# Order of the plain loads in the dense stage of an encoder block: raw second weights first, raw first weights one iteration behind the split, gate blocks by halves

## The chip, the cores and the metric

The kernel runs on one core of a Trainium2 chip. The metric is the device time of one execution in microseconds (us). PE is TensorE, DVE VectorE, ACT ScalarE, POOL GpSimd and SP SyncE; SP computes nothing here, it issues plain loads and stores as DMAs, one after the other in program order.

## What is computed

The reference is one encoder block over 1024 tokens of width 1024: a norm, a projection, attention beside a depthwise convolution, an output projection, and then an expert layer that the change is about. Its core is this:

```python
q = (xc @ peer_wq).reshape(TOKEN_CHUNK, PEER_HEADS, PEER_DQ)
...
v1, i1 = lax.top_k(s1, PEER_TOPK)
v2, i2 = lax.top_k(s2, PEER_TOPK)
...
g = jax.nn.softmax(top_s, axis=-1).astype(xc.dtype)
u = peer_u[e]
h = jax.nn.gelu(jnp.einsum('cd,chkd->chk', xc, u))
return jnp.einsum('chk,chkd->cd', g * h, peer_v[e])
```

Every token picks 128 of 16384 experts. An expert has a row of `peer_u` (the first weights), whose product with the token goes through a gelu and is scaled by a gate, and a row of `peer_v` (the second weights) that is added with this factor. All is float32; products on PE are made of three matmuls each on a rounded high part and a low rest of both operands.

## The kernel before

Of the eight tiles of 128 tokens, three are done by gathering: POOL fetches for each of the 128 choices of a tile the rows of `peer_u`, later of `peer_v`, by an indirect DMA (L1162, 512 KB each) into one of seven slots, and DVE works a slot off with one instruction (L1195 for the dot products, L1207 for the sums). A slot is fetched anew when DVE is done with it. The other five tiles (640 tokens) are done densely, over all 128 chunks of 128 experts. For chunk i:

- first product: PE multiplies the chunk of first weights with the normed tokens (`uhalf`, L1504) into the bank `hps`, ACT makes the gelu (L1514) into a buffer `ho`. The raw weights `ur` are loaded by `uload` (L1226) into one of two buffers and split by `usplit` (L1236): ACT makes the high part `uh` (L116), POOL the rest `ul` (L119). For 33 of the chunks this product was made earlier; their `ho` is loaded by `hload` (L1481).
- gate: DVE multiplies `ho` with the gate block `gl`, in two halves of the tokens (`amake1`, L1487); ACT rounds it to `ah` (L1489), DVE makes the rest `al` (L1495). A gate block holds four chunks and comes in two halves of 640 KB (`gload`, L1461), which share three buffers.
- second product: `vload` (L1465) loads the raw second weights `vr` into one of two buffers, `vsplit` has ACT make `vh` (L116) and POOL `vl` (L119); PE multiplies `ah`, `al` with them (L122 to L124). Four of the ten output blocks stay in PSUM banks (`acc`), the other six go in turns of two chunks through one bank `prot`, from which DVE adds to `X` (L1569).

The dense stage is the loop `for i in range(NK - 1)` at L1608, 127 iterations. The order within an engine is that of the program's text; each engine waits on semaphores for what an instruction needs. So SP issues the loads strictly in order, and a load whose buffer is not free yet holds up those behind it. Iteration i emits the loads for chunk i + 2, splits the second weights of chunk i + 1, and splits first weights in three of four iterations. The calls stand like this, with the gate block inside `loads` ahead of `vload` every fourth time, and the next `uload` inside `uahead`, behind the split that frees its buffer:

```python
            loads(i + 2)
            vsplit(nx)
            uahead()
```

Of the kernel before, what the change touches and what calls it, by code (L numbers as in the profile page):

```python
# [31 lines left out]
NK = 128  # L32
# [8 lines left out]
GCH = 4  # L41
# [30 lines left out]
def peer_block(tc, I, out):  # L72
# [1151 lines left out]
    def uload(i):  # L1224
        raw = uu.tile([P, DC, P], F32, name="ur", tag="raw", bufs=2)
        SY.dma_start(raw[:], I["peer_uT"][i])  # L1226
        RAW["u", i] = raw
# [4 lines left out]
    def usplit(i):  # L1232
        raw = RAW.pop(("u", i))
        uh = uu.tile([P, DC, P], F32R, name="uh", tag="uh", bufs=2)
        ul = uu.tile([P, DC, P], F32R, name="ul", tag="ul", bufs=2)
        split(uh[:], ul[:], raw[:], hi_eng=HE(i), lo_eng=V if i in UI and UI[i] > KM else G)  # L1236
        UW[i] = (uh, ul)
# [189 lines left out]
    with ExitStack() as vs:  # L1427
# [27 lines left out]
        AL = {}  # L1455
        HO = {}

        def gload(i):
            for hf in range(2):
                gl[i, hf] = vp.tile([P, NB2, GCH, TB], F32, name="gl", tag="gl", bufs=3)  # L1460
                SY.dma_start(gl[i, hf][:], GD[hf * NB2:(hf + 1) * NB2, :, i:i + GCH, :].rearrange("b p i t -> p b i t"))  # L1461

        def vload(i):
            raw = vp.tile([P, D], F32, name="vr", tag="vr", bufs=RB)
            SY.dma_start(raw[:], I["peer_v"][i * P:(i + 1) * P, :])  # L1465
            RAW["v", i] = raw

        def vsplit(i):
            raw = RAW.pop(("v", i))
            vh = vp.tile([P, D], F32R, name="vh", tag="vh", bufs=WIN + 1)  # L1470
            vl = vp.tile([P, D], F32R, name="vl", tag="vl", bufs=WIN + 1)
            split(vh[:], vl[:], raw[:], lo_eng=G)
            CH[i] = (vh, vl)
# [4 lines left out]
        def hload(i):  # L1478
            if i in UI and i not in HO and i < NK:
                HO[i] = hfree.pop(0)  # L1480
                SY.dma_start(HO[i], HDm[UI[i]])  # L1481

        def amake1(i):
            ho = HO[i]
            for hf in range(2):
                o = ho[:, hf * HT_:(hf + 1) * HT_].rearrange("p (b t) -> p b t", t=TB)
                V.tensor_tensor(o, o, gl[i - i % GCH, hf][:, :, i % GCH, :], op=ALU.mult)  # L1487
            ah = vp.tile([P, TD], F32R, name="ah", tag="ah", bufs=WIN + 1)
            A.copy(ah[:], ho)  # L1489
            AL[i] = ah  # L1490

        def amake2(i):
            ho = HO.pop(i)
            al = vp.tile([P, TD], F32R, name="al", tag="al", bufs=WIN + 1)
            V.tensor_tensor(al[:], ho, f(AL[i][:]), op=ALU.subtract)  # L1495
            AL[i] = (AL[i], al)
            hfree.append(ho)

        def uhalf(i, hf, ps, d0=0, d1=DC):
            a, b = segs[hf]  # L1500
            uh, ul = UW[i]
            for dc in range(d0, d1):
                for st3 in range(3):
                    PE.matmul(ps[:, :b - a], (uh, uh, ul)[st3][:, dc, :], HN[(0, 1, 0)[st3]][:, dc, a:b],  # L1504
                              start=dc == 0 and st3 == 0, stop=dc == DC - 1 and st3 == 2)
            if hf and d1 == DC:
                UW.pop(i)

        def ubank():
            return psv.tile([P, 512], F32, name="hps", tag="h", bufs=1)  # L1510

        def ugelu(ho, hf, ps):
            a, b = segs[hf]
            A.activation(ho[:, a:b], ps[:, :b - a], AF.Gelu_apprx_tanh)  # L1514

        def loads(i):
            if 0 <= i < NK:
                if i % GCH == 0:
                    gload(i)
                vload(i)  # L1520


        ulist = [i for i in range(NK) if i not in UI]
        ug = dict(g=0, split=0, load=0, ps=None)

        def uahead():
            m = ug["g"] // 4
            if ug["split"] < min(m + 2, len(ulist)):
                usplit(ulist[ug["split"]])
                ug["split"] += 1  # L1530
                if ug["load"] < len(ulist):
                    uload(ulist[ug["load"]])
                    ug["load"] += 1

        def ugroup():
            m, q = divmod(ug["g"], 4)
            if m >= len(ulist):
                return
            i, (hf, d) = ulist[m], divmod(q, 2)
            if ug["split"] <= m:  # L1540
                uahead()
            if d == 0:
                ug["ps"] = ubank()
            uhalf(i, hf, ug["ps"], d * DC // 2, (d + 1) * DC // 2)
            if d == 1:
                if hf == 0:
                    HO[i] = hfree.pop(0)
                ugelu(HO[i], hf, ug["ps"])
            ug["g"] += 1

        def uready(i):
            while i not in UI and ulist.index(i) >= ug["g"] // 4:
                ugroup()
# [4 lines left out]
        def rotate(w, i, wide):  # L1558
            t, n = rot[w]
            todo = list(range(last[w] + 1, i + 1))  # L1560
            last[w] = i
            if not todo:
                return
            pr = (ubank() if wide else psv.tile([P, 512], F32, name="prot", tag="r", bufs=1))[:]
            for c in todo:
                ah, al, vh, vl = *AL[c], *CH[c]
                mm3(pr, ah[:, t * P:(t + 1) * P], al[:, t * P:(t + 1) * P], vh[:, n:n + 512],
                    vl[:, n:n + 512], c == todo[0], c == i)
            V.tensor_tensor(X[:, NG + t, n:n + 512], X[:, NG + t, n:n + 512], pr, op=ALU.add)  # L1569
# [8 lines left out]
        ug["load"] = 2  # L1578
        hload(0)
        loads(0)  # L1580
        loads(1)
        for i in range(KM, K0):
            if i + 1 < K0:
                usplit(US[i + 1])
            else:
                amake1(0)
                amake2(0)
                vsplit(0)
                uahead()
            ho = vp.tile([P, TD], F32, name="hm", tag="al", bufs=WIN + 1)[:]  # L1590
            for hf in range(2):
                hps = ubank() if hf == 0 else psv.tile([P, 512], F32, name="prot", tag="r", bufs=1)
                uhalf(US[i], hf, hps)
                ugelu(ho, hf, hps)
            SY.dma_start(HDm[i], ho)

        def accum(i, js):
            ah, al, vh, vl = *AL[i], *CH[i]
            for j in js:
                t, n = pers[j]  # L1600
                mm3(acc[j][:], ah[:, t * P:(t + 1) * P], al[:, t * P:(t + 1) * P], vh[:, n:n + 512],
                    vl[:, n:n + 512], i == 0, i == NK - 1)
# [5 lines left out]
        for i in range(NK - 1):  # L1608
            nx = i + 1
            ng = gat0 + -(-(ngat - gat0) * min(nx, nb) // nb) - gat.nc  # L1610
            gs = [0] * 3
            for j in range(ng):
                gs[SPOTS[j % len(SPOTS)]] += 1
            hload(nx)
            if len(hfree) > 1:
                hload(i + 2)
            loads(i + 2)
            vsplit(nx)
            uahead()
            rs_ = [w for w in range(len(rot)) if i % WIN == w % WIN]  # L1620
            rotate(rs_[0], i, False)
            accum(i, (0,))
            ugroup()
            gat.adv(gs[0])
            rotate(rs_[1], i, False)
            accum(i, (1,))
            ugroup()
            uready(nx)
            amake1(nx)
            gat.adv(gs[1])  # L1630
            amake2(nx)
            rotate(rs_[2], i, False)
            accum(i, (2, 3))
            ugroup()
            gat.adv(gs[2])
            CH.pop(i - WIN, None)
# [72 lines left out]
```

## Time and profile before

| what | value |
|---|---|
| median of three runs | 2976.93 us (2971.88 to 2979.38) |
| the profiled execution's own time | 2979.52 us |
| span of its trace | 2977.7 us |
| busy: PE, DVE, POOL, ACT | 94%, 81%, 64%, 39% |
| moved by DMA | 710.33 MB, mean 239 GB/s |
| the dense stage in the trace | from about 1360 to 2950 us |

The shares are over the whole span, in which stages with different limits follow each other; for the dense stage the rows below are taken from its own stretch. "Busy" of PE counts matmuls whose ends are modelled, so its pace is read better from the starts of its rows.

### The profile page before, as it was taken

The numbers are of one execution on the slowest core, as the hardware profiler recorded it, in microseconds if no ns is written. First come the engines' busy times: TensorE is split into PE (matmuls) and PEld (weight loads), VectorE is DVE, ScalarE is ACT, GpSimd is POOL, SyncE is SP. The second block draws the span as 40 slices with busy tenths as digits, with TensorE's granted clock in tenths as the row PEclk, the third lists the DMA queues.
The fourth block names the chain that finished last, engine by engine and source line by source line (L and its number), as shares of the span: only waits on it lengthen the run. The fifth ranks groups of instructions, "written<-read, shape, count | busy, mean of one in ns | idle before, by whom it ended". The sixth has DMA issues, their size and how long they took to land.

```text
span 2977.7 us, 44502 instructions
## 1 busy us (share of the span) xinstructions
PE 2799.5 (94%) x16042; PEld 2477.2 (83%) x16048; DVE 2424.8 (81%) x4465; ACT 1166.3 (39%) x2408; POOL 1916.8 (64%) x1526
## 2 busy tenths in 40 slices
PE   7988899999999899978999999999999999999997
PEld 6867787798988788857888888888888888888886
DVE  4889877458666977766899988999889989898998
ACT  3237666243577577672222222222222222222222
POOL 2667741104446666765777777878777878787775
PEclk9999999899999999999999999999999999999999
DMA  3121000154345667668989898999989998999896
GB/s 124 53 76 36 1 15 1 53 161 122 96 149 181 224 219 251 235 238 299 342 331 350 328 348 331 345 342 352 337 319 337 344 343 336 347 336 339 332 342 227
DMA packets 296719, 710.33 MB, mean 239 GB/s; under 512 B 25264, under 2 KB 135216, under 8 KB 296368
## 3 DMA queue, kind: packets, MB, share of 16 engines
q0 software_dynamic: 110592, 402.70, 35.3%
q1 hardware_dynamic: 156800, 252.85, 25.2%
q10 hardware_dynamic: 29104, 51.91, 4.7%
q8 instruction: 126, 2.06, 0.3%
q14 instruction: 97, 0.79, 0.1%
HBM read 640.46 MB, written 66.91 MB: 238 GB/s over the span
## 4 chain that ended last, share of the span: by engine, by line
PE 53%; DVE 20%; DMA 11%; issue 7%; ACT 4%; POOL 4%; ACTq 1%; SPq 0%; POOLq 0%; DVEq 0%
PE hps L1504 13%; PE hps L1244 5%; PE prot L122 4%; PE prot L123 4%; PE prot L124 4%; DMA rows<-peer_u,ei 4%; PE pg L1108 3%; DMA rows<-peer_v,ei 2%; PE acc L124 2%; PE acc L122 2%; PE acc L123 2%; DMA vr<-peer_v 2%; DVE ga L1207 2%; DVE ho L1487 2%; DMA GD<-gblk 2%
## 5 line engine op out<-in xcount | busy, mean ns | idle before, releaser
L1504 PE MATMUL hps<-HN,uh 128*128 128x320 f32 x3072 | 682.8, 309 | 9.3 <-ACT ho L1251 5.3
L1504 PEld LDWEIGHTS hps<-HN,uh 128*128 128x128 f32 x3072 | 530.3, 188 | 42.7 <-issue 5.5
L1504 PE MATMUL hps<-HN,ul 128*128 128x320 f32 x1536 | 475.4, 309 | 0.6 <-POOL ul L119 0.6
L1207 DVE SCALAR_TENSOR_TENSOR ga<-rows,aa,ga 128x1024 f32<-128x1024 f32 x330 | 423.8, 1284 | 30.1 <-DMA rows<-peer_v,ei 23.6
L1162 POOL DMA_INDIRECT rows<-peer_u,ei x339 | 362.4, 1069 | 108.0 <-issue 56.3
L119 POOL TENSOR_TENSOR vl<-vr,vh 128x1024 fp32r<-128x1024 f32 x128 | 308.9, 2413 | 153.3 <-ACT vh L116 110.7
L1162 POOL DMA_INDIRECT rows<-peer_v,ei x330 | 325.2, 985 | 112.9 <-issue 64.5
L1195 DVE SCALAR_TENSOR_TENSOR QB<-rows,ga 128x1024 bf16<-128x1024 f32 x271 | 329.4, 1216 | 29.8 <-DMA rows<-peer_u,ei 25.5
L122 PE MATMUL prot<-vh,ah 128*128 128x512 f32 x762 | 308.8, 405 | 30.4 <-DVE X L1569 27.9
L119 POOL TENSOR_TENSOR ul<-ur,uh 128x1024 fp32r<-128x1024 f32 x127 | 323.0, 2543 | 2.6
L1569 DVE TENSOR_TENSOR X<-X,prot 128x512 f32<-128x512 f32 x384 | 261.9, 682 | 68.6 <-PE prot L124 66.4
L123 PE MATMUL prot<-vl,ah 128*128 128x512 f32 x762 | 301.0, 395 | 0.4 <-POOL vl L119 0.4
L124 PE MATMUL prot<-vh,al 128*128 128x512 f32 x762 | 297.4, 390 | 0.0
L1504 PEld LDWEIGHTS hps<-HN,ul 128*128 128x128 f32 x1536 | 289.1, 188 | 0.9 <-POOL ul L119 0.9
L1514 ACT ACTIVATE ho<-hps 128x320 f32<-128x320 f32 x128 | 55.9, 437 | 487.2 <-PE hps L1504 487.2
L1118 ACT COPY gblk<-pg 128x128 f32<-128x128 f32 x640 | 176.0, 441 | 100.6 <-PE pg L1108 71.4
L116 ACT CAST vh<-vr 128x1024 fp32r<-128x1024 f32 x128 | 133.7, 1045 | 201.7 <-DMA vr<-peer_v 201.7
L1244 PE MATMUL hps<-HN,uh 128*128 128x320 f32 x992 | 210.8, 335 | 0.0
L124 PE MATMUL acc<-vh,al 128*128 128x512 f32 x512 | 199.8, 390 | 0.0
L122 PE MATMUL acc<-vh,ah 128*128 128x512 f32 x512 | 199.8, 390 | 0.0
L123 PE MATMUL acc<-vl,ah 128*128 128x512 f32 x512 | 199.7, 390 | 0.0
L122 PEld LDWEIGHTS prot<-vh,ah 128*128 128x128 f32 x762 | 143.0, 188 | 67.9 <-DVE X L1569 47.6
(276 smaller groups left out, 6502.9 us busy)
## 6 DMA issues: line engine op xcount, KB each, us to landing
ur<-peer_uT SPq DMA_DIRECT2D x128, 512.0 KB, 4.4
vr<-peer_v SPq DMA_DIRECT2D x128, 512.0 KB, 7.8
GD<-gblk ACTq DMA_DIRECT2D x80, 512.0 KB, 5.1
gl<-GD SPq DMA_DIRECT2D x64, 640.0 KB, 7.7
wqr<-peer_wq SPq DMA_DIRECT2D x32, 512.0 KB, 3.9
HDm<-ho SPq DMA_DIRECT2D x31, 320.0 KB, 2.9
s<-SD SPq DMA_DIRECT2D x64, 128.0 KB, 3.0
ho<-HDm SPq DMA_DIRECT2D x22, 320.0 KB, 5.0
```

What stands on the lines that cost most here:

```text
L116: A.copy(hi, src)
L119: lo_eng.tensor_tensor(lo, src, f(hi), op=ALU.subtract)
L122: PE.matmul(ps, ah, bh, start=start, stop=False)
L123: PE.matmul(ps, ah, bl, start=False, stop=False)
L124: PE.matmul(ps, al, bh, start=False, stop=stop)
L1118: A.copy(gblk[b][k][:, :, q * 4:q * 4 + 4].rearrange("p i t -> p t i"), pg[:, :, k * w:k * w + w])
L1162: G.indirect_dma_start(out=r, out_offset=None, in_=I["peer_v" if ph else "peer_u"], in_offset=bass.IndirectOffsetOnAxis(ap=ge[t][:, k:k + ...
L1195: V.scalar_tensor_tensor(jk, r, 1.0, h, op0=ALU.mult, op1=ALU.mult, accum_out=self.hh[t][:, k:k + 1])
L1207: V.scalar_tensor_tensor(to, r, self.aa[t][:, k:k + 1], to, op0=ALU.mult, op1=ALU.add)
L1244: PE.matmul(hps[:, j, :b - a], (uh, uh, ul)[st3][:, dc, :], HN[(0, 1, 0)[st3]][:, dc, a:b], start=dc == 0 and st3 == 0, stop=dc == DC - 1 ...
L1504: PE.matmul(ps[:, :b - a], (uh, uh, ul)[st3][:, dc, :], HN[(0, 1, 0)[st3]][:, dc, a:b], start=dc == 0 and st3 == 0, stop=dc == DC - 1 and ...
L1569: V.tensor_tensor(X[:, NG + t, n:n + 512], X[:, NG + t, n:n + 512], pr, op=ALU.add)
```

## The change

The instructions are the same, and so is their order on PE, DVE, ACT and POOL (rows differ only in line numbers and in the numbers of buffers). Only the order of SP's loads differs. The second weights now come ahead of the `hload` for chunk i + 2. The first weights have a call of their own, `uloads()`, ahead of the iteration's splits, where the buffer it needs was freed by a split of an earlier iteration. The gate block is loaded by halves, called behind the `amake1` of the last chunk of a block: then come the second half of the next block and the first half of the one after it. Two more calls, each one half, go ahead of the loop.

```diff
-        def gload(i):
-            for hf in range(2):
+        def gload(i, hf):
+            if i < NK:
                 gl[i, hf] = vp.tile([P, NB2, GCH, TB], F32, name="gl", tag="gl", bufs=3)
                 SY.dma_start(gl[i, hf][:], GD[hf * NB2:(hf + 1) * NB2, :, i:i + GCH, :].rearrange("b p i t -> p b i t"))
...
         def loads(i):
             if 0 <= i < NK:
-                if i % GCH == 0:
-                    gload(i)
                 vload(i)
...
             if ug["split"] < min(m + 2, len(ulist)):
                 usplit(ulist[ug["split"]])
                 ug["split"] += 1
-                if ug["load"] < len(ulist):
-                    uload(ulist[ug["load"]])
-                    ug["load"] += 1
+
+        def uloads():
+            if ug["load"] < min(ug["split"] + 2, len(ulist)):
+                uload(ulist[ug["load"]])
+                ug["load"] += 1
...
         hload(0)
         loads(0)
+        gload(0, 0)
+        gload(0, 1)
         loads(1)
+        gload(GCH, 0)
...
             hload(nx)
+            loads(i + 2)
             if len(hfree) > 1:
                 hload(i + 2)
-            loads(i + 2)
+            uloads()
             vsplit(nx)
             uahead()
...
             amake1(nx)
+            if nx % GCH == GCH - 1:
+                gload(nx + 1, 1)
+                gload(nx + 1 + GCH, 0)
             gat.adv(gs[1])
```

Within the loop, SP's order repeats every four iterations. `vr` are raw second weights, `ur` raw first weights, `gl` halves of gate blocks, `ho` or `QB` a first product made earlier. Before, one such period late in the stage stands like this:

```order
L1226 DMA ur<-peer_uT 128x1024
L1481 DMA ho_14274<-HDm 128x640
L1465 DMA vr<-peer_v 128x1024
L1461 DMA gl<-GD 128x10x128 x2
L1465 DMA vr<-peer_v 128x1024
L1226 DMA ur<-peer_uT 128x1024
L1465 DMA vr<-peer_v 128x1024
L1226 DMA ur<-peer_uT 128x1024
L1465 DMA vr<-peer_v 128x1024
```

And now, in the same place:

```order
L1465 DMA vr<-peer_v 128x1024
L1481 DMA ho_14274<-HDm 128x640
L1226 DMA ur<-peer_uT 128x1024
L1465 DMA vr<-peer_v 128x1024
L1461 DMA gl<-GD 128x10x128 x2
L1465 DMA vr<-peer_v 128x1024
L1226 DMA ur<-peer_uT 128x1024
L1465 DMA vr<-peer_v 128x1024
L1226 DMA ur<-peer_uT 128x1024
```

The `vr` directly behind the two `gl` used to be that of the chunk that opens the new gate block; it now stands ahead of them, and the one behind them is that of the next chunk. The two `gl` were the halves of one block and are now the second half of it and the first half of the block after it.

Ahead of the loop, SP's order before was this (`HDm<-hm` are stores of first products that are made there):

```order
L1226 DMA ur<-peer_uT 128x1024
L1481 DMA ho_14273<-HDm 128x640
L1461 DMA gl<-GD 128x10x128 x2
L1465 DMA vr<-peer_v 128x1024 x2
L1595 DMA HDm<-hm 128x640
L1226 DMA ur<-peer_uT 128x1024
L1595 DMA HDm<-hm 128x640
L1481 DMA ho_14274<-HDm 128x640
```

It is now:

```order
L1226 DMA ur<-peer_uT 128x1024
L1481 DMA ho_14273<-HDm 128x640
L1465 DMA vr<-peer_v 128x1024
L1461 DMA gl<-GD 128x10x128 x2
L1465 DMA vr<-peer_v 128x1024
L1461 DMA gl<-GD 128x10x128
L1598 DMA HDm<-hm 128x640 x2
L1481 DMA ho_14274<-HDm 128x640
```

One `vr` moved ahead of the first gate block, half a gate block was added ahead of the stores, and the `ur` between the stores left this place for one inside the loop.

## Rows read from the trace of the kernel before

**Rows 1.** Windows: length, busy time by engine, clock, DMA share, GB/s; one stretch.

```profile
1900.00:2000.00 100.00, 99.97 (x539) 88.72 (x538) 91.59 (x139) 24.29 (x35) 79.93 (x60) 1.00 0.93 343
```

**Rows 2.** Windows of iterations 106 to 109 and 111, from first acc matmul to the next.

```profile
2690.64:2702.78 12.14, 12.14 (x68) 10.90 (x67) 10.27 (x12) 2.19 (x4) 10.15 (x8) 1.00 0.77 277
2702.78:2715.03 12.25, 12.25 (x68) 10.90 (x66) 11.38 (x11) 4.37 (x7) 8.42 (x6) 1.00 0.89 343
2715.03:2728.03 13.00, 12.62 (x67) 10.90 (x66) 12.07 (x13) 3.14 (x5) 11.00 (x10) 1.00 0.93 346
2728.03:2740.18 12.15, 12.15 (x68) 10.90 (x67) 11.15 (x13) 2.36 (x4) 9.14 (x8) 1.00 1.02 380
...
2752.32:2766.06 13.74, 12.65 (x67) 10.82 (x66) 12.87 (x11) 4.71 (x7) 8.40 (x6) 1.00 0.81 308
```

**Rows 3.** Timeline of PE in iteration 106: start, us, tile.

```profile
2691.32 0.45 PE L1504 MATMUL hps<-HN,uh 128*128 128x320 f32 x2
...
2693.07 0.39 PE L122 MATMUL prot<-vh,ah 128*128 128x512 f32 x1
...
2695.14 0.45 PE L1504 MATMUL hps<-HN,uh 128*128 128x320 f32 x2
```

**Rows 4.** Timeline of SP: start, us including the wait; first, typical and last gate blocks.

```profile
1370.27 25.23 SPq L1461 DMA_DIRECT2D gl<-GD  x2
...
2674.33 22.11 SPq L1461 DMA_DIRECT2D gl<-GD  x2
2696.53 0.60 SPq L1465 DMA_DIRECT2D vr<-peer_v  x1
2697.24 0.38 SPq L1226 DMA_DIRECT2D ur<-peer_uT  x1
2697.66 0.67 SPq L1465 DMA_DIRECT2D vr<-peer_v  x1
...
2874.42 21.66 SPq L1461 DMA_DIRECT2D gl<-GD  x2
```

**Rows 5.** Timeline of ACT, iterations 107 and 108; in brackets the idle time before.

```profile
2704.42 1.05 ACT L116 CAST vh<-vr 128x1024 fp32r<-128x1024 f32 x1 [6.27 <-DMA vr<-peer_v]
...
2714.06 1.04 ACT L116 CAST vh<-vr 128x1024 fp32r<-128x1024 f32 x1
2715.00 1.05 ACT L116 CAST uh<-ur 128x1024 fp32r<-128x1024 f32 x1
```

**Rows 6.** Timeline of POOL, iterations 106 to 108.

```profile
2693.27 2.42 POOL L119 TENSOR_TENSOR ul<-ur,uh 128x1024 fp32r<-128x1024 f32 x1
...
2701.36 0.93 POOL L1162 DMA_INDIRECT rows<-peer_v,ei  x1 [0.30 <-issue]
2705.55 2.41 POOL L119 TENSOR_TENSOR vl<-vr,vh 128x1024 fp32r<-128x1024 f32 x1 [3.25 <-ACT vh L116]
2707.90 2.67 POOL L119 TENSOR_TENSOR ul<-ur,uh 128x1024 fp32r<-128x1024 f32 x1
...
2717.98 2.42 POOL L119 TENSOR_TENSOR vl<-vr,vh 128x1024 fp32r<-128x1024 f32 x1
```

**Rows 7.** Timeline of DVE, iterations 106 to 109.

```profile
2695.26 1.18 DVE L1487 TENSOR_TENSOR QB<-QB,gl 128x320 f32<-128x320 f32 x2
...
2707.40 3.52 DVE L1487 TENSOR_TENSOR ho<-ho,gl 128x320 f32<-128x320 f32 x2
...
2718.76 1.29 DVE L1207 SCALAR_TENSOR_TENSOR ga<-rows,aa,ga 128x1024 f32<-128x1024 f32 x1 [0.82 <-DMA rows<-peer_v,ei]
...
2732.71 0.89 DVE L1487 TENSOR_TENSOR QB<-QB,gl 128x320 f32<-128x320 f32 x2
```

**Rows 8.** Waits by engine from 1395 to 2900 us: total, times, longest.

```profile
ACT vh L116 <- DMA vr<-peer_v: 194.3, 30, 7.9
...
POOL vl L119 <- ACT vh L116: 105.0, 52, 4.8
```

**Rows 9.** Timeline of DVE ahead of the loop.

```profile
1355.50 0.49 DVE L1487 TENSOR_TENSOR ho<-ho,gl 128x320 f32<-128x320 f32 x1 [8.35 <-DMA gl<-GD]
1357.46 0.49 DVE L1487 TENSOR_TENSOR ho<-ho,gl 128x320 f32<-128x320 f32 x1 [1.47 <-DMA gl<-GD]
```

## The prediction, made before the changed kernel had run

> **What bounds the kernel now.** I first looked for the stage that the change touches. In the dense stage PE hardly rests: in a good stretch it is busy for 99.97 of 100 us, with DVE at 91.59 and the DMA engines at 0.93 [rows 1]. So the question is how far an iteration is from PE's own pace. That pace is read from the starts of PE's rows: twelve `hps` matmuls take 2693.07 - 2691.32 = 1.75 us, nine of the second product 2695.14 - 2693.07 = 2.07 [rows 3]. An iteration has three groups of twelve and 30 matmuls of the second product (three rotations of six, four `acc` of three): 3 x 1.75 + 30 x 0.23 = 12.15. Iterations 106 and 109 run at that floor, 12.14 and 12.15; 107 and 108 take 12.25 and 13.00, 111 takes 13.74 [rows 2].
>
> Next, the period. The gate blocks come every four iterations, and each pair blocks SP until DVE frees a buffer. The first pair of the loop ends at 1370.27 + 25.23 = 1395.50, the thirtieth after it at 2874.42 + 21.66 = 2896.08 [rows 4]. A period is (2896.08 - 1395.50) / 30 = 50.02 us. Four floor iterations are 48.56, so 1.46 us are lost per period, and over 127 iterations (31.75 periods) 46.4 us. That is all that a better order of loads can give: the instructions stay, and PE can't go below its pace.
>
> Then I asked who is late in each period. SP sits at the gate blocks from 2674.33 to 2696.44. The `vr` behind them, that of chunk 108, is issued at 2696.53 [rows 4]; ACT has idled 6.27 us when it casts it at 2704.42 [rows 5]; POOL, free at 2701.36 + 0.93, has waited 3.25 us when it starts `vl` at 2705.55 [rows 6]. That happens in every period: 30 waits of ACT, 194.3 us in all, 6.5 each; POOL waits 105.0 us for it [rows 8].
>
> Neither is the bound, but both reach PE. POOL's late `ul` lies from 2707.90 to 2710.57 [rows 6] over DVE's gate product, which then takes 3.52 us where it takes 0.89 undisturbed [rows 7]. POOL's fetches start after that `ul`, so its next `vl` starts 2.95 us into iteration 108, at 2717.98 against a start at 2715.03 [rows 2, 6], and DVE waits 0.82 us for a fetched row [rows 7]. DVE's addition to `X` is then late, the one bank `prot` is not free, and PE stops in iterations 107, 108 and 111.
>
> **The change part by part.**
>
> *Second weights ahead of the gate block.* The buffer that `vr` of chunk 108 needs is that of chunk 106, split an iteration before the gate block's buffers come free. So this `vr` is now issued more than an iteration earlier, and has landed long before its cast. ACT's 6.5 us and POOL's 3.25 us go. POOL, free at 2702.29, does `vl` and `ul` in 2 x 2.41 us and ends at 2707.1, ahead of the gate product at 2707.40 [rows 6, 7]. DVE gets back 3.52 - 0.89 = 2.63 us in this iteration and part of the 0.82 in the next.
>
> The rows show an overlap of DVE's gate product with POOL's split. [...]
>
> *First weights one iteration behind.* `ur` is now issued behind the splits of the iteration before, and in one iteration of four behind the gate blocks. Its queue there: two halves of 640 KB, a `vr`, itself: 2.36 MB. Before, gate half and `vr` (1.18 MB) were there 2704.42 - 2696.06 = 8.4 us after the first issue (issue at the end of the wait, 2696.44 less its own 0.38; I take 0.38 from the next row of SP) [rows 4, 5], so this queue moves some 141 GB/s beside the fetches. Then `ur` lands 16.7 us after 2696.06, at 2712.8. It is cast at 2715.00 now [rows 5]. POOL, 3.25 us earlier than today, would start `vl` at 2714.7 and `ul` at 2717.1, so the cast must begin by 2716.0: 3.2 us to spare. The `vr` ahead of it (1.84 MB, 13.0 us, 2709.1) is cast at 2714.06 [rows 5]. Cost nothing, with this cover; if it is gone, see the third rival. The other `ur` stand behind no blocked load.
>
> *Gate block by halves.* The half that is needed next is issued when the same gate product as now frees its buffer, and is first in the burst as now. Its use is an iteration later. No cost. The other half moves from a quiet place into the burst, in place of a `vr`: burst before 640 + 3 x 512 KB, now 2 x 640 + 2 x 512, 8% more. Bounds for what this does to the fetches: nothing, or all of DVE's 0.82 us of waiting on a row [rows 7].
>
> *Ahead of the loop.* One `vr` now stands ahead of the first gate block, for which DVE waits 8.35 us with nothing else to do; the two halves land 1.96 us apart [rows 9]. The `vr` is 0.8 of a half: between 1.6 us (at that pace) and 3.7 us (at 141 GB/s). On the path: it delays the first iteration. I take 2.
>
> *Sum.* Lost per period 1.46 us. What remains afterwards lies between 0 (all iterations like 106 and 109) and 1.46. I take 0.4: waits for fetched rows behind the burst stay, since the burst stays. (1.46 - 0.40) x 31.75 = 33.7, less 2 ahead of the loop: 31.7 us. From the profiled execution's 2979.5 that makes 2947.8; the median of the runs is 2.6 lower, so 2945.2 is my time.
>
> **The rivals.**
>
> *The overlap only moves (2960).* POOL without waits is earlier everywhere, but its `vl` and `ul` take 4.8 of 12.14 us, and in iteration 106 `ul` ends at 2695.69, 0.43 us into a gate product that begins at 2695.26 and takes 1.18 [rows 6, 7]. So the room is under half a microsecond. Should the splits settle a microsecond later than in iteration 106, most gate products would run into them, and DVE has little slack (91.59 of 100, [rows 1]). Then about half of the loss stays: 0.73 x 31.75 - 2 = 21, or, with one more such overlap per period, 15 us of gain. I name 2960, by the middle.
>
> *The burst, not the `vr`, sets the loss (2977).* If DVE and PE are late because rows fetched during the burst are late, the order inside the burst is nothing. For it: iteration 108 has DVE's wait for a row. Against: the 0.82 us there is small beside the 2.63 of the gate product, and iteration 109 has the highest DMA share, 1.02, and runs at the floor [rows 2].
>
> *First weights late (about 3000, slower).* The place is the split of iteration 108. If the burst moves slower than 141 GB/s, POOL waits for the cast of `ur` where it now waits for that of `vr`. It decides at 3.2 us of lateness for a cost at all and at 3.2 + 3.25, thus landing at 2719.3 (101 GB/s), for as much as today. At 95 GB/s it lands at 2720.9, POOL waits some 4.9 us, and the loss grows to 1.46 x 4.9 / 3.25 = 2.2 per period: 0.74 x 31.75 + 2 = 25 us slower. For it: all queues together move 343 GB/s in a good stretch [rows 1]; five to six fetches of 512 KB per 12.14 us are some 230 of it by my estimate, and at the 113 left `ur` would land at 2717.0 and cost POOL 1 us. Against: 141 is what the burst itself showed.
>
> **How the numbers follow.** My case (gain of 20 to 46 us) 0.68, overlap moved 0.15, burst 0.10, first weights late 0.07. The whole 46.4 us would give 2930.5, a small scatter of runs 2929; upward the range takes in the second case up to 2969. That leaves out the cases of no gain, 0.17. The likeliest one's own range is 2929 to 2957. A difference of 0.3% (8.9 us) is about what a measurement tells from none; the three runs lie 7.5 us apart. Faster by more than that: the first two cases, 0.82, with 0.01 off for a smaller gain; same 0.11; slower 0.07.
>
> **What would show it.** Right: ACT's wait for `vr` under 30 us in all; POOL's for `vh` under half of 105; the gate product near 1 us in most iterations; periods of gate blocks near 49 us; SP's wait at the gate blocks shorter, with a `vr` ahead of them. Wrong: ACT waiting for `ur` in its place (third rival), gate products still of 2 us and more (first), or DVE's waits for rows as before with PE still late behind the burst (second). Also wrong would be the first iteration starting over 4 us later than before.

## The result and the profile after

The changed kernel takes 2935.54 us (median of five runs, 2932.07 to 2938.54) against 2971.88 (five runs, 2969.84 to 2979.38) of the kernel before on the same chip: ratio 0.9871, 95% interval 0.9851 to 0.9891. It is 36.3 us faster; 31.7 had been forecast. The forecast time, 2945.2, lies 9.7 us above the measured one; 5.0 of them are that the median before is 2971.88 of five runs, where the forecast started from 2976.93 of three. The span of the profiled execution fell from 2977.7 to 2936.8 us, by 40.9.

Where the time came from is seen in the windows of iterations 106 to 109 and 111, the ones of [rows 2]. The columns are the stretch, its length, busy time of PE, PE's weight loads, DVE, ACT and POOL, the granted clock, the DMA share and GB/s. The last row is of iteration 104.

```profile
2656.42:2668.56 12.14, 12.14 (x68) 10.90 (x66) 10.27 (x12) 4.08 (x6) 10.61 (x9) 1.00 0.68 223
2668.56:2680.70 12.14, 12.14 (x68) 10.90 (x66) 10.83 (x12) 2.35 (x4) 10.18 (x8) 1.00 1.04 399
2680.70:2692.84 12.14, 12.14 (x68) 10.90 (x66) 9.88 (x12) 3.14 (x5) 10.61 (x9) 1.00 1.03 408
2692.84:2704.98 12.14, 12.14 (x68) 10.90 (x66) 10.83 (x12) 2.35 (x4) 8.18 (x7) 1.00 0.95 364
...
2717.12:2729.26 12.14, 12.14 (x68) 10.90 (x66) 10.83 (x12) 2.35 (x4) 10.18 (x8) 1.00 1.03 397
...
2630.81:2644.28 13.47, 12.41 (x68) 10.90 (x66) 12.97 (x13) 4.41 (x6) 10.12 (x8) 1.00 0.97 365
```

The first five run at PE's floor of 12.14; iteration 104, where DVE goes over from the dot products of a gathered tile (L1195) to its sums (L1207), is one of three from the third iteration on that do not (the others are 34 and 36). DVE's busy time in iterations 107 and 108 fell from 11.38 and 12.07 [rows 2] to 10.83 and 9.88.

The whole stage is measured on PE's timeline, from the first row of `acc` in the loop's first iteration to the first of its last one. Columns: start, us, engine, line, operation.

```profile
1366.28 0.63 PE L122 MATMUL acc<-vh,ah 128*128 128x512 f32 x1
...
2899.22 0.39 PE L122 MATMUL acc<-vh,ah 128*128 128x512 f32 x1
```

That is 1532.94 us, 3.3 above 126 x 12.14 = 1529.6. In the kernel before the same two rows are these:

```profile
1362.92 0.40 PE L122 MATMUL acc<-vh,ah 128*128 128x512 f32 x1
...
2940.19 0.39 PE L122 MATMUL acc<-vh,ah 128*128 128x512 f32 x1
```

That is 1577.27 us, 47.6 above the floor. The stage became 44.3 us shorter and starts 3.4 later.

What happens around iteration 107 now (it starts at 2668.56), by the timeline of SP, ACT, POOL and DVE (in brackets the idle time before, and what ended it):

```profile
2661.85 1.08 SPq L1461 DMA_DIRECT2D gl<-GD  x2
2663.03 2.32 SPq L1465 DMA_DIRECT2D vr<-peer_v  x1
2665.44 1.36 SPq L1226 DMA_DIRECT2D ur<-peer_uT  x1
...
2663.82 1.05 ACT L116 CAST vh<-vr 128x1024 fp32r<-128x1024 f32 x1
...
2668.11 2.42 POOL L119 TENSOR_TENSOR vl<-vr,vh 128x1024 fp32r<-128x1024 f32 x1
2670.47 2.41 POOL L119 TENSOR_TENSOR ul<-ur,uh 128x1024 fp32r<-128x1024 f32 x1
...
2673.18 0.89 DVE L1487 TENSOR_TENSOR ho<-ho,gl 128x320 f32<-128x320 f32 x2
```

ACT casts `vr` at 2663.82 with no wait, where it had idled 6.27 us [rows 5]; POOL starts `vl` without the 3.25 us of [rows 6] and ends `ul` at 2672.88, 0.3 us before the gate product, which takes 0.89 where it took 3.52 [rows 7].

The waits from 1395 to 2860 us, the loop without its last iterations ([rows 8] go 40 us further, since that stage ended later; engine, line, what ended the wait; total, times, longest):

```profile
DVE X L1569 <- PE prot L124: 110.7, 156, 1.7
...
POOL vl L119 <- ACT vh L116: 21.5, 27, 2.2
DVE X L1569 <- issue: 20.6, 37, 1.0
...
DVE QB L1195 <- DMA rows<-peer_u,ei: 11.9, 18, 1.8
...
DVE ga L1207 <- DMA rows<-peer_v,ei: 5.4, 6, 1.3
...
ACT uh L116 <- DMA ur<-peer_uT: 3.1, 3, 1.3
```

ACT's 194.3 us of waiting for `vr` are gone from the list, SP's for a gate buffer fell from 441.5 + 207.3 us to 315.0 + 147.1, POOL's for `vh` fell from 105.0 to 21.5, and a new wait of ACT, for `ur`, is 3.1 us in all. DVE now waits for PE 131.3 us over 1465 us (first and third row; the third names nothing that ended it, and I take it for the same), 1.09 per iteration: that is its slack on average. In single iterations it is 12.14 less the busy time above, 1.31 us in 107 and 2.26 in 108.

The kernel before had these in the same stretch:

```profile
DVE X L1569 <- PE prot L124: 58.1, 92, 2.0
...
DVE QB L1195 <- DMA rows<-peer_u,ei: 24.2, 27, 2.3
...
DVE ga L1207 <- DMA rows<-peer_v,ei: 23.0, 23, 3.3
PE prot L122 <- DVE X L1569: 16.4, 39, 1.9
```

The last one, PE held up by DVE's addition to `X`, is 2.4 us now:

```profile
PE prot L122 <- DVE X L1569: 2.4, 3, 1.1
```

DVE's gate products have two names, `ho` and `QB`. In the same stretch they took this before (number, busy us, mean ns):

```profile
L1487 DVE TENSOR_TENSOR ho<-ho,gl 128x320 f32<-128x320 f32 x158 | 162.1, 1065 | 0.0
L1487 DVE TENSOR_TENSOR QB<-QB,gl 128x320 f32<-128x320 f32 x78 | 78.8, 1050 | 0.0
```

And now:

```profile
L1487 DVE TENSOR_TENSOR ho<-ho,gl 128x320 f32<-128x320 f32 x162 | 89.4, 592 | 0.0
L1487 DVE TENSOR_TENSOR QB<-QB,gl 128x320 f32<-128x320 f32 x80 | 43.8, 587 | 0.0
```

So the gate products alone take 240.9 - 133.2 = 107.7 us less of DVE. Part of it came out as the 44 us of PE's stage, part as DVE's longer waits for PE.

### The profile page after: what moved, and what is told of

Its sections match the earlier page's. It is cut to its first block, busy times and chain, and to the rows that moved or that the text cites. A ratio compares the mean times of both kernels' runs of the same rounds, so it can differ in the third digit from the quotient of the medians.

```text
span 2936.8 us, 44533 instructions
## 1 busy us (share of the span) xinstructions
PE 2782.6 (95%) x16048; PEld 2480.3 (84%) x16048; DVE 2320.7 (79%) x4465; ACT 1163.4 (40%) x2408; POOL 1921.2 (65%) x1526
## 3 DMA queue, kind: packets, MB, share of 16 engines
q0 software_dynamic: 110592, 402.70, 36.3%
## 4 chain that ended last, share of the span: by engine, by line
PE 74%; DVE 13%; ACT 4%; DMA 3%; issue 3%; POOL 2%; ACTq 1%; SPq 0%; POOLq 0%; DVEq 0%
PE hps L1504 22%; PE prot L123 6%; PE prot L122 6%; PE prot L124 6%; PE hps L1244 5%; PE acc L124 4%; PE acc L122 4%; PE acc L123 4%; PE pg L1108 3%; DVE y L151 2%; DVE ac L151 1%; DVE PT L119 1%; DVE mx L711 1%; ACT gblk L1118 1%; PE pqT L122 1%
## 5 line engine op out<-in xcount | busy, mean ns | idle before, releaser
L1207 DVE SCALAR_TENSOR_TENSOR ga<-rows,aa,ga 128x1024 f32<-128x1024 f32 x330 | 424.2, 1285 | 12.9 <-DMA rows<-peer_v,ei 5.4
L1162 POOL DMA_INDIRECT rows<-peer_v,ei x330 | 336.1, 1019 | 126.1 <-issue 61.0
L1195 DVE SCALAR_TENSOR_TENSOR QB<-rows,ga 128x1024 bf16<-128x1024 f32 x271 | 329.7, 1216 | 17.9 <-DMA rows<-peer_u,ei 11.9
L122 PE MATMUL prot<-vh,ah 128*128 128x512 f32 x762 | 301.0, 395 | 12.5 <-DVE X L1569 10.6
L122 PE MATMUL acc<-vh,ah 128*128 128x512 f32 x512 | 199.4, 390 | 0.0
L1108 PE MATMUL pg<-o,o 128*128 128x128 f32 x1280 | 174.2, 280 | 11.1 <-ACT gblk L1118 9.0
L1108 PEld LDWEIGHTS pg<-o,o 128*128 128x128 f32 x1280 | 166.1, 196 | 17.4 <-ACT gblk L1118 11.1
```

The lines of the kernel that those rows point to most:

```text
L122: PE.matmul(ps, ah, bh, start=start, stop=False)
L1108: PE.matmul(pg[:, j, :], o2[:, j, :], o1[:, j, :], start=True, stop=True)
L1162: G.indirect_dma_start(out=r, out_offset=None, in_=I["peer_v" if ph else "peer_u"], in_offset=bass.IndirectOffsetOnAxis(ap=ge[t][:, k:k + ...
L1195: V.scalar_tensor_tensor(jk, r, 1.0, h, op0=ALU.mult, op1=ALU.mult, accum_out=self.hh[t][:, k:k + 1])
L1207: V.scalar_tensor_tensor(to, r, self.aa[t][:, k:k + 1], to, op0=ALU.mult, op1=ALU.add)
```

## The experiments

The theory going in was the prediction's: the `vr` behind the gate halves makes ACT and then POOL late, POOL's split lies over the gate product, DVE is held up and PE with it. Rivals: that other parts of the change bring the gain; that ACT's wait itself is what counts; that late fetches of rows, not the overlap, hold DVE up. Every kernel ran five to twelve times beside the kernel before. "Stage" is from the start of the first to that of the very last `acc` row of L122 in the profiled execution; "gate" is the sum of the gate products from 1395 to 2860 us.

| kernel | median us | ratio to before (95%) | stage us | gate us |
|---|---|---|---|---|
| before | 2971.88 | 1 | 1588.4 | 240.9 |
| changed | 2935.54 | 0.9871 (0.9851 to 0.9891) | 1544.1 | 133.2 |
| e1_vr_first | 2938.59 | 0.9866 (0.9848 to 0.9883) | 1545.3 | 132.9 |
| e2_ur_behind | 2978.55 | 1.0006 (0.9993 to 1.002) | 1583.5 | 255.9 |
| e3_vr_between | 2973.51 | 0.9985 (0.9974 to 0.9996) | 1583.1 | 241.2 |
| e4_pool_late | 2967.26 | 0.997 (0.996 to 0.998) | 1576.0 | 260.4 |
| e10_pool_write_ahead | 2973.29 | 0.9997 (0.9981 to 1.0012) | 1583.2 | 269.6 |
| e5_pool_read_behind | 2955.15 | 0.9939 (0.9917 to 0.9961) | 1561.5 | 220.5 |
| e6_pool_write_behind | 2950.48 | 0.9939 (0.9916 to 0.9962) | 1561.5 | 180.3 |
| e9_split_late | 2987.3 | 1.0043 (1.0028 to 1.0057) | 1599.0 | 256.6 |
| e7_ur_later | 2948.86 | 0.9911 (0.9887 to 0.9936) | 1555.9 | 146.7 |
| e8_gate_first | 2933.58 | 0.9865 (0.9841 to 0.989) | 1544.4 | 131.7 |

The median of the kernel before was 2978.14 beside e1 to e4, 2973.16 beside e5 to e8, 2972.91 beside e9 and e10; these three groups ran on three chips, so kernels of different groups are compared by their ratios. The ratios are worked out over all runs, not from the medians alone.

### Which part of the change brings it

**e1_vr_first** is the kernel before with the opening chunk's `vr` ahead of its two gate halves, and nothing else:

```diff
             if 0 <= i < NK:
+                vload(i)
                 if i % GCH == 0:
                     gload(i)
-                vload(i)
```

> The kernel before with one swap: the second weights of the chunk that opens a gate block stand ahead of the two gate halves; first weights and gate halves stay where they were. My theory (the late second weights are the whole loss): iterations at 12.14 us, 30 to 38 us faster than the kernel before, ratio 0.987 to 0.990, ACT's wait for vr near 0. Rival (the gate halves or the first weights had a share): 10 to 25 us faster, ratio 0.992 to 0.997.

It has the whole gain, and the same stage length within 1.2 us. **e2_ur_behind** is the kernel before with only the first weights' load moved ahead of the splits:

```diff
                 ug["split"] += 1
-                if ug["load"] < len(ulist):
-                    uload(ulist[ug["load"]])
-                    ug["load"] += 1
...
             loads(i + 2)
+            uloads()
             vsplit(nx)
```

> The kernel before with the first weights alone moved ahead of the iteration's splits; the second weights stay behind the gate halves. My theory: no gain, ratio 0.998 to 1.002, ACT waits for vr as before, some 190 us. Rival (the order of the first weights gives part of the gain): ratio below 0.997.

Nothing that the medians tell: ACT waits 190.0 us for `vr` as before. **e3_vr_between** is the changed kernel with the opening chunk's `vr` put between the two gate halves, so behind the one whose buffer is late:

```diff
-            loads(i + 2)
+            if (i + 2) % GCH:
+                loads(i + 2)
...
                 gload(nx + 1, 1)
+                loads(nx + 1)
                 gload(nx + 1 + GCH, 0)
```

> The changed kernel, with the second weights of the chunk that opens a gate block issued between its two gate halves, where they stood in time before: the rest of the new order stays. My theory: the loss of 1.4 us per period comes back, ratio 0.998 to 1.003, ACT waits for vr 190 us and more. Rival (the burst or the gate halves made the gain): the ratio stays at 0.987.

Nearly the whole loss is back, with the waits of [rows 8], here again from 1395 to 2860 us:

```profile
ACT vh L116 <- DMA vr<-peer_v: 198.2, 37, 8.2
...
POOL vl L119 <- ACT vh L116: 106.5, 48, 5.2
```

So of all that the change moves, one load in four iterations does the work: the `vr` of the chunk that opens a gate block. The order of the first weights brings nothing that e2 can tell. Together with the gate block by halves it brings little at most: e3 has both and is 0.15% faster than the kernel before (0.04 to 0.26).

### Is it ACT, or POOL?

**e4_pool_late** is the changed kernel with POOL alone made late: three additions on a buffer of its own (128x448, 0.94 us each) ahead of the splits of every fourth iteration.

```diff
+        dz = vp.tile([P, 448], F32, name="dz")
+        V.memset(dz[:], 0.0)
...
             uloads()
+            if nx % GCH == 0:
+                for _ in range(3):
+                    G.tensor_tensor(dz[:], dz[:], dz[:], op=ALU.add)
             vsplit(nx)
```

> The changed kernel with three additions of 128x448 on POOL ahead of the split of each chunk that opens a gate block (32 times, some 3.5 us each time, on a scratch tile that nothing reads): POOL as late as before, ACT on time. My theory (POOL's lateness over DVE's gate product stops PE): most of the loss comes back, ratio 0.994 to 1.000, gate products of 2 us and more in that iteration. Rival (ACT's late gelu stopped PE): no loss, ratio at 0.987 to 0.989.

**e10_pool_write_ahead** has six memsets in that place instead (3.1 us in all), which read nothing:

```diff
+                for _ in range(6):
+                    G.memset(dz[:], 0.0)
             vsplit(nx)
```

> The changed kernel with six POOL memsets (some 3.1 us in all, they read nothing) ahead of the splits in every fourth iteration: the lateness of the run with three additions in the same place, made of instructions that by themselves did not hold DVE's gate product up. Splits and fetches are both late, as in the kernel before, while ACT is on time. If the splits' lateness and what follows from it set the loss, this comes out as the run with additions ahead did, 2960 to 2970, with gate products near 1.1 us on average. If it was the additions' own reading that cost DVE time there, it comes out with the runs that put work behind the splits, 2946 to 2956.

POOL's lateness alone brings back most of the loss in e4 (ratio 0.997) and all of it in e10 (0.9997), although ACT is on time (no wait for `vr` in either). That the additions' own reading had done it in e4 is ruled out by e10. ACT's lateness by itself may have a small part, which was not tested alone: in e3 and before, PE also waits for a gelu of ACT in a few places (2.0 + 1.4 us in e3's list of waits), in e4 and e10 nowhere.

### Is it the overlap with the gate product, or late fetches?

Late splits also make the fetches behind them late: in iteration 107 of the kernel before the first one behind `ul` starts at 2710.72, 3.32 us behind the start of the gate product, in the changed kernel at 2673.04, 0.14 ahead of it. **e5_pool_read_behind** and **e6_pool_write_behind** put the same work behind both splits, so that the splits are on time and the fetches are not (in e6 `ul` ends at 2679.63 and the first fetch behind it starts at 2682.93, with the product at 2679.94); e5's additions lie over the gate product, e6's memsets too, but read nothing.

```diff
             vsplit(nx)
             uahead()
+            if nx % GCH == 0:
+                for _ in range(3):
+                    G.tensor_tensor(dz[:], dz[:], dz[:], op=ALU.add)
```

(e6 has six `G.memset(dz[:], 0.0)` there.)

> The changed kernel with the same three additions on POOL (0.94 us each in the run before) once per gate block, but behind both splits of that iteration: the splits end before DVE's gate product begins, the additions lie over it, and the row fetches start 2.8 us late as with the additions ahead. Theory of the overlap (what stops PE is a POOL instruction that reads SBUF and lies over the gate product): the gate product of that iteration loses at most about one addition, 1 us, instead of 2.8; the next iteration's split, behind the late fetches, still runs into its gate product; a part of the loss comes back, ratio 0.989 to 0.994. Theory of the late fetches alone (DVE waits for rows): the same loss as with the additions ahead, ratio 0.996 to 0.998.

> As the run with three additions behind the splits, but with six writes of a constant on POOL (128x448, each of unknown length, no input read) in their place. If only POOL instructions that read SBUF hold DVE's gate product up, the product of that iteration stays at 1 us, and what is lost comes from the next iteration alone: for a total length near 2.8 us a ratio of 0.988 to 0.993. If any POOL instruction holds it up, the gate product shows 2 us and more and the ratio is that of the additions or above.

Both lost about 17 us of stage, less than half, and equally much. POOL and DVE in the same iteration, e5 first:

```profile
2687.98 3.22 POOL L1628 TENSOR_TENSOR dz<-dz 128x448 f32<-128x448 f32 x3
...
2688.34 2.07 DVE L1487 TENSOR_TENSOR ho<-ho,gl 128x320 f32<-128x320 f32 x2
```

And e6:

```profile
2679.55 3.13 POOL L1628 MEMSET dz<- 128x448 f32 x6
...
2679.94 0.89 DVE L1487 TENSOR_TENSOR ho<-ho,gl 128x320 f32<-128x320 f32 x2
```

Additions under the product, which read `dz`, make it 2.07 us; memsets, which only write it, leave it at 0.89. They differ in operation and length too (1.02 and 0.47 us each on average), and which of these differences does it was not shown.

But the times are equal, so these 1.2 us in one iteration cost nothing: they are within DVE's slack there, 1.31. What both kernels lose comes later. In the next iteration POOL is still late and its splits lie over the next gate product (that is why e6 has 180.3 us of gate products and not 133). By itself that costs an iteration like 108 in most periods only 0.1 to 0.2 us: in e6 it takes 12.28, with a product of 2.45. More of the 17 us stands elsewhere by the starts of the `acc` rows: some 7 in every fourth iteration from 45 to 85, two behind the added work, and 5 to 6 in iterations 8, 12, 36 and 104. Why there was not followed up.

Whether late fetches do it can be read from DVE's waits for rows (`rows`, L1195 and L1207, 1395 to 2860 us). They are 47.2 us in the kernel before and 47.5 in e6, but 9.6 in e4 and 9.0 in e10, which lose 32 and 39 us of stage where e6 loses 17. So late rows are not what most of the loss needs.

After e5 and e6 I held for a moment that the overlap in the first iteration is harmless in general. **e9_split_late** tests that: the changed kernel, with the splits of that iteration behind its first fetches, and no instruction added.

```diff
-            vsplit(nx)
-            uahead()
+            if nx % GCH:
+                vsplit(nx)
+                uahead()
...
             gat.adv(gs[0])
+            if nx % GCH == 0:
+                vsplit(nx)
+                uahead()
```

> The changed kernel with one move on POOL, ACT and nothing else: in the iteration that used to be late (every fourth, the one that splits the second weights of a block-opening chunk) both splits are emitted behind the iteration's first fetches instead of ahead of them. So POOL reaches its splits two to three us later, its additions run into the gate product, and no fetch is later than in the changed kernel when the iteration ends. This parts two things that were always joined so far, the overlap of split and gate product and the lateness of the fetches behind it. If the overlap is what loses (the prediction's step, about 2.6 us of DVE in each period), gate products of 2 us and more stand in that iteration and 15 to 30 us come back: 2950 to 2966. If the overlap alone is harmless because DVE has slack in that iteration, and the loss needs late fetches and the next iteration's late split, the time stays within 6 us of the changed kernel (2936): 2932 to 2942, although the gate products of that iteration are as long.

It is slower than the kernel before, by more than either reading had forecast. POOL and DVE in iteration 107 of e9:

```profile
2706.28 2.41 POOL L119 TENSOR_TENSOR vl<-vr,vh 128x1024 fp32r<-128x1024 f32 x1 [0.86 <-ACT vh L116]
2708.64 2.66 POOL L119 TENSOR_TENSOR ul<-ur,uh 128x1024 fp32r<-128x1024 f32 x1
...
2706.75 4.90 DVE L1487 TENSOR_TENSOR ho<-ho,gl 128x320 f32<-128x320 f32 x2
```

And that iteration and the next, as windows:

```profile
2702.13:2715.72 13.59, 12.41 (x67) 10.90 (x66) 12.71 (x11) 4.79 (x7) 9.10 (x7) 1.00 1.04 398
2715.72:2728.50 12.78, 12.43 (x67) 10.90 (x66) 12.67 (x13) 2.92 (x4) 10.99 (x9) 1.00 0.98 336
```

The two halves of the gate product take 4.90 us instead of 0.89, and the second ends 0.35 us behind `ul` (2711.65 against 2711.30). The loads for these splits come in time (for the next two ACT waits 0.40 and 0.51 us), and the iteration's first fetches are ahead of them; `vl` starts 4.15 us after the iteration's start where it was 0.45 ahead of it (2668.11 against 2668.56). DVE waits for rows only 3.5 us in the whole stretch. Yet PE loses 1.45 us in this iteration and 0.64 in the next, and by its waits over the stretch it is held up by DVE's addition to `X` and nothing else:

```profile
PE prot L122 <- DVE X L1569: 41.2, 49, 1.9
```

So the overlap alone is enough. How much of it PE can bear is seen beside e10, whose iterations 107 and 108 are these (the product of 107, then the windows of both):

```profile
2697.26 3.36 DVE L1487 TENSOR_TENSOR ho<-ho,gl 128x320 f32<-128x320 f32 x2
...
2692.64:2704.78 12.14, 12.14 (x67) 10.90 (x66) 11.26 (x11) 2.35 (x4) 10.91 (x11) 1.00 1.03 398
2704.78:2717.95 13.17, 12.67 (x68) 10.90 (x66) 13.06 (x13) 3.25 (x5) 11.34 (x9) 1.00 0.95 347
```

The product of 107 is 2.47 us longer than undisturbed, and that iteration still takes 12.14; the next product takes 3.26, 2.37 longer, and its iteration loses 1.03. In the changed kernel DVE's room in these two iterations is 1.31 + 2.26 = 3.57 us. e5 puts 1.18 + 1.48 = 2.66 of longer products into it and loses 0.13; e10 puts 2.47 + 2.37 = 4.84 and loses 1.03; e9 puts 4.01 + 0.92 = 4.93, most of it into the tighter iteration, and loses 2.09.

The last two columns of the table say the same roughly: below 135 us of gate products nothing is lost, from 180 to 220 some 17 us, from 240 up 32 to 55. It is not a straight line, since it counts where the overlaps lie.

### The margin of the first weights, and the start

**e7_ur_later** puts `ur`, in the one iteration of four where it stands behind the gate halves, behind one more `vr`:

```diff
-            uloads()
+            if nx % GCH:
+                uloads()
+            if nx % GCH == 1:
+                uloads()
```

> The changed kernel with the first weights that stand behind the gate halves put one more second-weight load back, so that they are issued some 5 us later, in the iteration ahead of their split. By the prediction's margin of 3.2 us they come some 3 us too late for POOL: ACT waits for ur about 4 us once per period, and half to all of the loss comes back, ratio 0.992 to 1.000. If there is more room than I worked out: ratio stays at 0.987.

```profile
ACT uh L116 <- DMA ur<-peer_uT: 91.6, 26, 8.9
...
POOL ul L119 <- ACT uh L116: 55.1, 20, 7.5
```

By e7's list of waits over the same stretch ACT now waits for `ur`, POOL for ACT, and about 12 us of stage are lost, a quarter of the loss, where half to all of it had been expected. By the starts of the `acc` rows nearly all of the 12 us stand in iterations 49 to 81. The third rival's mechanism is real, and in that part of the stage the changed kernel stands close to it.

**e8_gate_first** is the changed kernel with the first gate block ahead of the first `vr`, in front of the loop (where three calls of `gload` stand now, one half each; one call brought both halves before):

```diff
-        loads(0)
         gload(0, 0)
         gload(0, 1)
+        loads(0)
         loads(1)
```

> The changed kernel with the first gate block ahead of the first second weights again, in front of the loop only. The prediction's term for this place is 2 us: the first gate product starts 1.6 to 3.7 us earlier after the load of the first product ahead of it, and the time is 2 us lower than the changed kernel, ratio 0.986 to 0.987, which a ratio can hardly tell. Rival: the first matmul of the loop waits for the second weights' low part instead, and nothing is won.

From the issue of the last `ur` ahead of the loop to the first `acc` row it takes 1361.21 - 1344.72 = 16.49 us, the changed kernel 1366.28 - 1348.97 = 17.31, the kernel before 1362.92 - 1347.18 = 15.74. So the place of the first gate block is worth 0.8 us at the first `acc` row, and 0.35 at the third iteration's (41.32 us behind the same `ur` against 41.67). The ratios, 0.9865 and 0.9871, don't tell the two apart.

## Why the prediction was right

**Right: the bound and the floor.** 47.6 us above the floor were measured over the stage; the prediction had worked out 46.4 from the blocks' period. The floor is reached: from the third iteration on all but three take 12.14 to 12.17.

**Right: the chain.** `vr` late, ACT late, POOL late, split over gate product, DVE late, PE late. e1 and e3 show that it starts at `vr`, e10 that POOL's lateness is enough without ACT's, e9 that the overlap is enough without late fetches, and that PE then waits for DVE. Even the places fit: POOL was to be done ahead of the product, by 2707.1 against 2707.40; it is done 0.3 us ahead (2672.88 against 2673.18). The gate product of [rows 7] ends 0.35 us behind `ul` (2707.40 + 3.52 = 2710.92 against 2710.57 [rows 6]), as in e9.

**Mis-sized: what remains.** The term that failed in size is "What remains afterwards lies between 0 (all iterations like 106 and 109) and 1.46. I take 0.4". From the third iteration on (first `acc` row at 1390.64) the stage takes 2899.22 - 1390.64 = 1508.58 us, 3.2 above 124 x 12.14 = 1505.4: 0.10 per period, and nearly all of it in three iterations, 34, where the gathering goes over to another tile, 36 behind it, and 104, where it goes over to its sums (13.47). The reason given for 0.4, "waits for fetched rows behind the burst stay, since the burst stays", was wrong: the burst stayed, and DVE's waits for rows fell from 24.2 + 23.0 us to 11.9 + 5.4. With the same burst and later fetches they are 26.3 + 21.2 (e6), and 5.8 + 3.2 where DVE itself is late (e10), so they hang on when POOL fetches and when DVE comes, not on the burst. (0.40 - 0.10) x 31 = 9.3 us is nearly the whole difference between the forecast gain in the stage, 33.7, and the measured 44.3. The working has a slip beside it that changes no term: two halves of 640 KB and two loads of 512 KB are 6% more than 640 + 3 x 512 KB, not 8%.

**Right at the first `acc` row, gone by the third iteration: the start.** 2 us were taken; from the issue of `ur` to the first `acc` row it is 17.31 against 15.74, 1.6 more. On DVE the first gate product waits 9.63 us instead of 8.35 [rows 9]:

```profile
1358.57 0.49 DVE L1487 TENSOR_TENSOR ho<-ho,gl 128x320 f32<-128x320 f32 x1 [9.63 <-DMA gl<-GD]
1360.52 0.49 DVE L1487 TENSOR_TENSOR ho<-ho,gl 128x320 f32<-128x320 f32 x1 [1.45 <-DMA gl<-GD]
```

The other 1.8 us of the later start lie ahead of that `ur`, in stages that the change does not touch. In sum, 44.3 - 1.6 - 1.8 = 40.9, the difference of the spans. But the first two iterations take 24.36 us now and took 26.71 before, so at the third iteration the changed kernel is 41.67 us behind that `ur` and the kernel before 42.46. In these two executions the term of 2 us was lost at first and won back at once; which part of the new order won it back was not tested.

**Right, with less to spare than worked out: first weights.** 3.2 us of margin were estimated and no cost. ACT waits for `ur` three times, at most 1.3 us, so in some periods the margin is used up; one `vr` more in front of it costs 12 us (e7).

**The rivals.** That the overlap only moves didn't happen: the splits settled in a place where they end 0.3 us ahead of the product. e9 puts them over the product, but 4.6 us later, where this rival thought of one microsecond, and is slower than the kernel before; the price of 2960 was not tried. That the burst sets the loss is refuted: the burst is as the prediction described it (a DMA share of 1.04 and 1.03 in the windows of 107 and 108), and the loss is gone. First weights late came true only in e7.

**Left open.** How far the splits can slip before PE loses time is known at three sizes only, 1.2, 2.5 and 4.0 us of overlap in iteration 107. Why e5, e6 and e7 lose most of their time in some stretches of the stage and next to none in others was not followed up. The two parts of the change that brought little are together in e3 alone, with `vr` between the halves and not behind both.

## What to carry over

In a queue that issues in order, a load that waits for a buffer is a wait for all behind it (here 22.11 us at two gate halves, with the `vr` behind them issued at 2696.53 [rows 4]): put it behind those whose buffers are free already, even where it is used first, if it still comes in time. When an engine that is 91% busy loses time, look for what runs on other engines at that moment before looking at what it waits for: here POOL's lateness cost time by where its work landed (a gate product of 3.52 us with a split over it, of 0.89 without). And after such a move look for the next load that now has the least to spare.

## What was not expected

**The issue itself can take long.** Behind two gate halves SP needs 2.32 us for a `vr` and 1.36 for the next `ur`, where the next `vr` and `ur` take 0.33 each. In the kernel before a `vr` in that place took 0.60 [rows 4], behind halves that had waited for their buffers. Ahead of the loop, where a `vr` stands behind the first block, it is more:

```profile
1350.46 0.43 SPq L1465 DMA_DIRECT2D vr<-peer_v  x1
1350.93 1.10 SPq L1461 DMA_DIRECT2D gl<-GD  x2
1352.07 4.91 SPq L1465 DMA_DIRECT2D vr<-peer_v  x1
```

The list of SP's waits puts 72.4 us of its time at `vr`, in 19 waits, down to DMAs of second weights. Why was not tested; it costs the kernel nothing that was seen, but it delays what stands behind: the `ur` behind that `vr` is issued at 2665.44 only.

**The start of the stage scatters.** The last `ur` ahead of the loop was issued at 1349.0 us in the changed kernel and at 1338.9 in e9, with the same program ahead of it. That is 10 us between two profiled executions, and so one span by itself doesn't tell differences of that size; the stage lengths and the ratios over several runs do.
